# Narrow matmuls in a hybrid decoder trunk: value matmuls of two heads in alternate column halves, recurrence scores as 64x64 quarters

## The chip, the cores and the metric

The kernel runs on one core of one Trainium2 chip. The metric is the device time of one execution in microseconds; the kernel before takes 1604.14 us (median of 3 runs, 1604.09 to 1604.67). A core has a matmul engine (TensorE, PE in the profile, with its weight loads as PEld), three engines for elementwise work (VectorE is DVE, ScalarE is ACT, GpSimd is POOL) and DMA queues, here issued by SyncE (SP). TensorE's array has 128 rows and 128 columns; a matmul loads a stationary operand ("weights") and streams a moving one past it, and writes to PSUM, which the other engines then read.

## The reference

Two layers over 256 tokens of width 1024, batch 1, all in float32. Each layer is: x = LN(a x + half SwiGLU); x = LN(a x + W_o sum of three gated mixers); x = LN(a x + attention over 256 memory tokens); x = LN(a x + half SwiGLU). The three mixers share one input projection:

- A, native sparse attention: 8 heads of 64 channels in two key groups; compressed, selected and sliding branches. At 256 tokens all blocks of the selection and the whole window are in reach, so selected and sliding are two causal attentions with keys and values of their own.
- B, a gated linear recurrence (HGRN2) with 4 heads of 128 channels: out(t) = sum over s <= t of a(t, s) v(s), with a(t, s) = sum over channels of q(t) k(s) exp(b(t) - b(s)), where b is the running sum of the logarithms of the forget gates.
- C, multi-head latent attention with 8 heads, causal.

The change concerns the scores a(t, s) of B, and the sums of weights times values of A and C:

```
a = einsum('bhtd,bhtsd,bhsd->bhts', qt, decay, kt);  intra = einsum('bhts,bhse->bhte', a, vt)
o_sel = einsum('bgtrkl,bgtkld->bgtrd', p, vg);  o_win = einsum('bnqgrk,bnkgd->bnqgrd', p_w, vwb)
o (MLA) = einsum('bhqk,bkhd->bqhd', p, v)
```

## The kernel before

Tokens are two tiles of 128 (NT = 2, S = 256). The large projections multiply split operands in three float32r matmuls each (`mm3`, lines 126 to 129); the small matmuls of the mixers are plain float32, which the chip runs as two passes, so that the trace has two weight loads and two matmuls for each of them. Weights stream in from memory in blocks (`wblock`) and are split into a high and a low part by ScalarE (line 77) and VectorE (line 78).

The order of work is not the order of the text. The program is written down once in textual order, and a planner (line 1201) then orders each engine's queue with a timing model: it sends what is ready, and of several ready instructions the textually first. Instructions of the text can thus be sent ahead of others that wait. Semaphores follow from the tiles' uses. Buffers come from pools: m4 ("big", 10 tiles of 4 KB per partition), m2 ("half", 8 of 2 KB), PSUM pools `pw` and `acc` of 4 banks each, and the tag "pT" with 2 buffers.

`mixer` (from line 461) runs the recurrence first. `fT`, `kT`, `qT` hold gates, keys and queries with channels on partitions. Scores inside blocks of four tokens are made first (lines 579 to 584): for each token tile and head a 128x128 matmul `lv`, multiplied by a mask into `at[t]`, which holds scores with keys on partitions and queries along the row. Then `level(i, m)` for m = 4, 8, 16, 32, 64 (lines 596 to 612) adds the pairs of neighbouring blocks of m tokens: again 8 matmuls of 128x128, each token tile copied under a mask (line 604), then keys and queries are multiplied by the block's decay for the next level. Level 4 follows the masks at once; each of the other levels stands behind one more projection (`proj_nat`, PSUM name `pn`). Pairs between the two token tiles are one more product, `atx` (line 664). `hgrn_out` multiplies `at` and `atx` with the values.

The attention of A and C goes in 12 units (lines 928 to 955): 8 heads of A with their two branches, then 4 units of C with two heads each. A unit runs some filler units (projections of gates and branches, PSUM names `mg` and `br`; the counts are `FILLS`, line 34), turns the weights of its head or heads (`flip`, six transposes of p into PSUM name `pt`, copied to the two halves of pT by ScalarE, line 448, and VectorE, line 450), computes scores and softmax of the unit two ahead (`soften_a`, `soften_c`), and then applies its own weights to the values with `weigh` (line 453): per branch or head two matmuls with 64 columns of weights (the values), one with 256 streaming columns (line 454) and one with 128 (line 455). Their output is 64 partitions of a PSUM tile of 128: even heads write partitions 0 to 63, odd heads 64 to 127, and so use the left or the right half of the array's columns. The accumulator `oa` of two heads is started by line 824 (the compressed branch, 128 columns); `oc` is that of C.

Of the kernel before, what the change touches and what calls it, by code (L numbers as in the profile page):

```python
# [12 lines left out]
I32 = mybir.dt.int32  # L13
U8 = mybir.dt.uint8
AF = mybir.ActivationFunctionType
# [19 lines left out]
LEVELS = (4, 8, 16, 32, 64)  # L35
C_ID, C_CAUS, C_BASE, C_HM, C_CM, C_CM1, C_INV, C_END = 0, 128, 384, 512, 520, 552, 584, 600


@with_exitstack
def trunk(ctx, tc, a, out):  # L40
# [13 lines left out]
    def big(shape, dt=F32, name="m"):  # L54
        return m4.tile(shape, dt, tag="m4", name=name)

    def half(shape, dt=F32, name="h"):
        return m2.tile(shape, dt, tag="m2", name=name)
# [21 lines left out]

    # weights that a LayerNorm's work on the same engines must not wait for
    held = []
# [60 lines left out]

# [1 line left out]
    cst = const.tile([P, C_END], F32, name="cst")  # L145
    msk = const.tile([P, 5, P], U8, name="msk")
    ident = cst[:, C_ID:C_ID + P]
    caus = cst[:, C_CAUS:C_CAUS + S]
    basem = cst[:, C_BASE:C_BASE + P]
    headm = cst[:, C_HM:C_HM + 8]  # L150
# [7 lines left out]
    def load_constants():  # L158
        nc.sync.dma_start(cst, a["cst"])
        mski = big([P, 5, P], I32, name="mski")  # L160
        nc.sync.dma_start(mski, a["msk"])
        V.tensor_copy(msk, mski)
        nc.sync.dma_start(vec, a["vec"])
        nc.sync.dma_start(w2k, a["w2k"])
        nc.sync.dma_start(w2v, a["w2v"])

# [1 line left out]
    def xT_tiles():  # L168
# [19 lines left out]

    # matmuls whose results nobody reads, so that the clock of TensorE is up when there is work again
    def warm(n, x):  # L190
# [13 lines left out]

# [1 line left out]
    cc16 = const.tile([P, NT, 16], F32, name="cc16")  # L206
# [46 lines left out]

# [1 line left out]
    lbt = const.tile([P, DEPTH, 4], F32, name="lbt")  # L255
# [24 lines left out]

# [1 line left out]
    def layer_norm(ys, l, i, last=False, idle=0):  # L282
# [55 lines left out]

# [1 line left out]
    def ffn(l, i, xT, first=None, then=(), pre=()):  # L340
# [53 lines left out]

# [1 line left out]
    def mem_k(l, memT, K32, c, w=None):  # L396
# [18 lines left out]

# [1 line left out]
    def soft(score, scale, gate=None):  # L417
# [34 lines left out]

    def weigh(o, v, pT, start):
        T.matmul(o, v[0], pT[:, 0:S], start=start, stop=False, skip_group_check=True)
        T.matmul(o[:, P:S], v[1], pT[:, S:S + P], start=False, stop=True, skip_group_check=True)

    kc_blk = const.tile([P, 2, 32], F32, name="kc_blk")
    V.memset(kc_blk, 0.0)

# [1 line left out]
    def mixer(l, xT, first, pre):  # L461
# [28 lines left out]

        # gated sum of the branch projections, in units of one weight block
        order = "bac"
# [48 lines left out]

        # HGRN2, channels on partitions
        fT, kT, qT = big([P, 4, S], name="fT"), big([P, 4, S], name="kT"), big([P, 4, S], name="qT")
# [15 lines left out]
        for h in range(4):  # L559
            ps = ppw([P, S], "zq")  # L560
            mode_b(ps, wblock(a["winb"][l, 4 + h]), xT)
            A.activation(qT[:, h, :], ps, AF.Copy)
        # sums of the logarithms within blocks of four tokens
        pairs = fT.rearrange("p h (n c) -> p (h n) c", c=2)
        V.tensor_tensor(pairs[:, :, 1:2], pairs[:, :, 1:2], pairs[:, :, 0:1], op=ALU.add)
        b4 = fT.rearrange("p h (n m) -> p (h n) m", m=4)
        V.tensor_tensor(b4[:, :, 2:4], b4[:, :, 2:4], b4[:, :, 1:2].to_broadcast([P, S, 2]), op=ALU.add)
        # pairs within those blocks, about the mean of the middle sums
        at = [half([P, 4, P], name="at") for _ in range(NT)]
        c2 = small([P, S], "c2")  # L570
# [7 lines left out]
        V.tensor_tensor(eq, eq, qT, op=ALU.mult)  # L578
        for t in range(NT):
            ps = ppw([P, 4, P], "lv")  # L580
            s = slice(t * P, (t + 1) * P)
            for h in range(4):
                T.matmul(ps[:, h, :], ek[:, h, s], eq[:, h, s], start=True, stop=True)
            V.tensor_tensor(at[t], ps, basem[:, None, :].to_broadcast([P, 4, P]), op=ALU.mult)
        # keys decayed to the end of their block, queries from the start of theirs, block by block twice as long
        dk = big([P, 4, S], name="dk")
# [9 lines left out]
        def level(i, m):  # L596
            nonlocal fm
            nb = 2 * S // m
            for t in range(NT):
                ps = ppw([P, 4, P], "lv")  # L600
                s = slice(t * P, (t + 1) * P)
                for h in range(4):
                    T.matmul(ps[:, h, :], kT[:, h, s], qT[:, h, s], start=True, stop=True)
                V.copy_predicated(at[t], msk[:, i, None, :].to_broadcast([P, 4, P]), ps)
            k3 = kT.rearrange("p h (n w m) -> p (h n) w m", w=2, m=m)
            q3 = qT.rearrange("p h (n w m) -> p (h n) w m", w=2, m=m)
            f3 = fm[:, 0:2 * nb].rearrange("p (n w) -> p n w", w=2)
            V.tensor_tensor(k3[:, :, 0, :], k3[:, :, 0, :], f3[:, :, 1:2].to_broadcast([P, nb, m]), op=ALU.mult)
            V.tensor_tensor(q3[:, :, 1, :], q3[:, :, 1, :], f3[:, :, 0:1].to_broadcast([P, nb, m]), op=ALU.mult)
            fm2 = small([P, S], "fm")  # L610
            V.tensor_tensor(fm2[:, 0:nb, None], f3[:, :, 0:1], f3[:, :, 1:2], op=ALU.mult)
            fm = fm2
# [3 lines left out]

        # NSA and MLA projections, tokens on partitions
        level(0, LEVELS[0])
# [40 lines left out]
        rsqrt(rkv, rkv, 1.0 / 256, RMS_EPS)  # L659
        # pairs between the two token tiles  # L660
        atx = half([P, 4, P], name="atx")
# [4 lines left out]

        # compressed keys and values
        ct = big([P, 4, S], name="ct")
# [36 lines left out]
        def hgrn_out(t):  # L705
            ps = ppw([P, 4, P], "ob")
            for h in range(4):
                hs = slice(h * P, (h + 1) * P)
                if t == 1:
                    T.matmul(ps[:, h, :], atx[:, h, :], vN[:, 0, hs], start=True, stop=False)  # L710
                T.matmul(ps[:, h, :], at[t][:, h, :], vN[:, t, hs], start=(t == 0), stop=True)
            ob = wk.tile([P, 4, P], F32, tag="p", name="obn")
# [63 lines left out]

        # queries and keys with channels on partitions
        qtu = big([P, 4, S], name="qtu")
# [25 lines left out]

        # selected and sliding attention, both at once for every head
        yah, yal = y_tiles("a")

        def soften_a(h):
# [9 lines left out]
            return soft(score, 1.0, gt[:, :, h, 1:3])  # L818

        def values_a(h, pT):  # L820
            j, r = h // 2, slice(h % 2 * 64, h % 2 * 64 + 64)
            if h % 2 == 0:
                oa[j] = pacc([P, S], "oa")
                T.matmul(oa[j], vc[:, 2 * j:2 * j + 2, :].rearrange("p h d -> p (h d)"), pc, start=True, stop=False,
                         skip_group_check=True)
            for br in range(2):
                weigh(oa[j][r], [vs[:, t, br * 2 + h // 4, :] for t in range(NT)], pT[:, br], False)
            if h % 2 == 1:
                evac_hl(yah[:, j, :], yal[:, j, :], oa[j])

        oa = {}
        # MLA
        qm, kf, vm = [], [], []
# [66 lines left out]
        def values_c(u, pT):  # L900
            o = pacc([P, S], "oc")
            for w in range(2):
                weigh(o[w * 64:(w + 1) * 64], [vm[t][:, 2 * u + w, :] for t in range(NT)], pT[:, w], True)
            evac_hl(ych[:, u, :], ycl[:, u, :], o)

        # compressed attention's weights, both tiles and all heads at once
        scm = small([P, NT, 8, 16], "scm")
# [66 lines left out]

# [1 line left out]
    def cross(l, xT, memT, K32, vx, first, pre):  # L976
# [140 lines left out]
def _constants():  # L1117
# [3 lines left out]
    c[:, C_CAUS + P:C_CAUS + S] = np.where(i[None, :] <= i[:, None], 0.0, NEG)  # L1121
    c[:, C_BASE:C_BASE + P] = (i[:, None] // 4 == i[None, :] // 4) & (i[:, None] <= i[None, :])
    c[:, C_HM:C_HM + 8] = i[:, None] // 16 == np.arange(8)[None, :]
# [5 lines left out]
    c[:, C_INV:C_INV + 16] = np.float32(ROPE_THETA) ** (-np.arange(16, dtype=np.float32) / np.float32(16))  # L1129
    m = np.zeros((P, 5, P), np.int32)  # L1130
    for k, w in enumerate(LEVELS):
        same = i[:, None] // (2 * w) == i[None, :] // (2 * w)
        m[:, k, :] = same & (i[:, None] // w % 2 == 0) & (i[None, :] // w % 2 == 1)
    return c, m
# [79 lines left out]
```

## Time and profile before

| | |
|---|---|
| runs | 1604.14 us median, 1604.09 to 1604.67 |
| profiled execution, first to last instruction (its own time as far as the profile shows it) | 1602.4 us |
| TensorE matmuls busy | 1583.2 us, 99% |
| TensorE weight loads busy | 1462.7 us, 91% |
| VectorE / ScalarE busy | 1046.2 us, 65% / 826.8 us, 52% |
| mean granted TensorE clock | 0.998 |
| DMA | 282.49 MB, mean 176 GB/s |

The profile is one execution. Records of matmuls overlap, since they are pipelined: the record of a matmul is longer than its share of the array, and what it occupies is read from one start to the next. In a timeline, instructions of one kind that follow each other are merged into one row with their count (x16). "128*64 128x256" means 128 rows and 64 columns of weights, and an operand of 128 partitions with 256 elements (for a matmul the streaming one, for a weight load the stationary one).

### The profile page before, as it was taken

The page shows a single profiled execution, that of the slowest core. Times are in us where ns is not written, and L with a number is a line of the kernel's source. Part 1 is how long each engine was busy: PE and PEld are TensorE (multiplying, and loading weights), DVE is VectorE, ACT ScalarE, POOL GpSimd, SP SyncE. Part 2 cuts the span into 40 slices and gives each one's busy share as a digit, 9 for nine tenths or more (in the row PEclk, how much of TensorE's full clock was granted, in tenths as well). Part 3 has the DMA queues.
Part 4 walks back from the last instruction along what each step waited for, and adds up shares of the span by engine and source line. Part 5 has one row for each costly group of instructions (what it writes and reads, how often), then busy time and mean ns, then how long its engine had stood idle before and what let it go on. Part 6 is the DMA issues. An engine that isn't in the chain of part 4 may idle for free.

```text
span 1602.4 us, 27351 instructions
## 1 busy us (share of the span) xinstructions
PE 1583.2 (99%) x10896; PEld 1462.7 (91%) x10896; DVE 1046.2 (65%) x1831; ACT 826.8 (52%) x1396; POOL 32.8 (2%) x32
## 2 busy tenths in 40 slices
PE   9999999999999999999999999999999999999997
PEld 8999998898898989999999999988989989899996
DVE  5585559778766776555565555787786677655555
ACT  5455365566564564445444454745575545454443
POOL 0000000000000000000000000000000000000000
PEclk9999999999999999999999999999999999999999
DMA  8677455562555464566646676446525545556562
GB/s 292 210 221 261 136 171 159 164 225 67 165 169 181 132 215 151 186 198 222 212 124 189 201 215 206 131 152 192 193 77 155 164 158 179 176 172 184 184 186 77
DMA packets 81199, 282.49 MB, mean 176 GB/s; under 512 B 9392, under 2 KB 10544, under 8 KB 81072
## 3 DMA queue, kind: packets, MB, share of 16 engines
q1 hardware_dynamic: 81072, 280.75, 55.1%
q8 instruction: 85, 1.39, 0.4%
q14 instruction: 42, 0.34, 0.1%
HBM read 279.67 MB, written 1.05 MB: 175 GB/s over the span
## 4 chain that ended last, share of the span: by engine, by line
PE 96%; DVE 1%; ACT 1%; DMA 1%; issue 0%; SPq 0%; POOLq 0%; POOL 0%; DVEq 0%; ACTq 0%
PE up L129 10%; PE up L127 10%; PE up L128 10%; PE y L127 7%; PE y L128 7%; PE y L129 7%; PE mg L127 3%; PE mg L128 3%; PE mg L129 3%; PE pn L127 3%; PE pn L128 3%; PE pn L129 3%; PE br L127 2%; PE br L129 1%; PE br L128 1%; PE up L138 1%
## 5 line engine op out<-in xcount | busy, mean ns | idle before, releaser
L78 DVE TENSOR_TENSOR wl<-raw,wh 128x1024 fp32r<-128x1024 f32 (+3 forms) x490 | 584.5, 1200 | 369.9 <-ACT wh L77 368.4
L77 ACT ACTIVATE wh<-raw 128x1024 fp32r<-128x1024 f32 (+3 forms) x490 | 504.6, 1039 | 517.1 <-issue 227.9
L127 PE MATMUL up<-xTh,wh 128*128 128x256 f32 x1360 | 384.8, 283 | 0.7 <-ACT xTh L77 0.6
L128 PE MATMUL up<-xTl,wh 128*128 128x256 f32 x1360 | 385.2, 284 | 0.0
L129 PE MATMUL up<-xTh,wl 128*128 128x256 f32 x1360 | 384.5, 283 | 0.0
L127 PEld LDWEIGHTS up<-xTh,wh 128*128 128x128 f32 x1360 | 260.8, 192 | 4.8 <-ACT xTh L77 1.3
L128 PEld LDWEIGHTS up<-xTl,wh 128*128 128x128 f32 x1360 | 260.9, 192 | 3.4 <-DVE xTl L78 0.4
L129 PEld LDWEIGHTS up<-xTh,wl 128*128 128x128 f32 x1360 | 260.7, 192 | 0.0
L128 PE MATMUL y<-wl,gh 128*128 128x512 f32 x352 | 137.3, 392 | 0.0
L127 PE MATMUL y<-wh,gh 128*128 128x512 f32 x352 | 136.9, 392 | 0.0
L129 PE MATMUL y<-wh,gl 128*128 128x512 f32 x352 | 135.7, 389 | 0.0
L127 PE MATMUL mg<-xTh,wh 128*128 128x256 f32 x384 | 110.1, 287 | 0.0
L128 PE MATMUL mg<-xTl,wh 128*128 128x256 f32 x384 | 109.5, 285 | 0.0
L129 PE MATMUL mg<-xTh,wl 128*128 128x256 f32 x384 | 108.8, 284 | 0.0
L129 PEld LDWEIGHTS y<-wh,gl 128*128 128x128 f32 x352 | 66.2, 188 | 14.3
L127 PEld LDWEIGHTS y<-wh,gh 128*128 128x128 f32 x352 | 66.4, 189 | 11.7
L128 PEld LDWEIGHTS y<-wl,gh 128*128 128x128 f32 x352 | 66.4, 189 | 10.9
L127 PEld LDWEIGHTS mg<-xTh,wh 128*128 128x128 f32 x384 | 73.5, 191 | 1.4 <-issue 1.4
L127 PE MATMUL pn<-wh,xTh 128*128 128x512 f32 (+1 forms) x192 | 74.3, 387 | 0.0
L129 PE MATMUL pn<-wh,xTl 128*128 128x512 f32 (+1 forms) x192 | 74.3, 387 | 0.0
L128 PE MATMUL pn<-wl,xTh 128*128 128x512 f32 (+1 forms) x192 | 74.3, 387 | 0.0
L128 PEld LDWEIGHTS mg<-xTl,wh 128*128 128x128 f32 x384 | 73.6, 192 | 0.4 <-issue 0.3
(406 smaller groups left out, 2879.7 us busy)
## 6 DMA issues: line engine op xcount, KB each, us to landing
raw<-in_w_dram SPq DMA_DIRECT2D x260, 512.0 KB, 4.2
raw<-in_winb_dram SPq DMA_DIRECT2D x64, 512.0 KB, 4.2
raw<-in_wina_dram SPq DMA_DIRECT2D x40, 512.0 KB, 3.7
raw<-in_wbr_dram SPq DMA_DIRECT2D x24, 512.0 KB, 4.3
raw<-in_wk_dram SPq DMA_DIRECT2D x16, 512.0 KB, 3.4
raw<-in_cw_dram SPq DMA_DIRECT2D x16, 512.0 KB, 4.2
raw<-in_wv_dram SPq DMA_DIRECT2D x16, 512.0 KB, 4.0
raw<-in_wq_dram SPq DMA_DIRECT2D x16, 512.0 KB, 4.4
```

Source lines behind the costliest of these rows:

```text
L77: i = A.activation(h, src, AF.Copy)
L78: j = V.tensor_tensor(l, src, f(h), op=ALU.subtract)
L127: T.matmul(o, lhs[0], rhs[0], start=start, stop=False)
L128: T.matmul(o, lhs[0], rhs[1], start=False, stop=False)
L129: latest[0] = T.matmul(o, lhs[1], rhs[0], start=False, stop=stop)
L138: T.matmul(o, w[i][:, k * P:(k + 1) * P], rhs[j][:, k], start=n + k == 0, stop=(n, k) == (2, nk - 1))
```

## The change

The values: `weigh` takes a list of two (output, values, weights) and issues the two 256-column matmuls, then the two 128-column ones. In A, `values_a` of an even head only keeps its pT; at the odd head the accumulator is started and both heads are weighed, branch by branch. In C the two heads of a unit are given to one `weigh`.

The recurrence: pairs inside 64 tokens are computed by `within` as matmuls of 64 keys by 64 queries. The two quarters on the diagonal of a 128x128 block go one after the other, with keys and output on partitions 0 to 63 and then 64 to 127 of one PSUM tile, for all 8 pairs of token tile and head. One masked operation then takes all of them (`near` is the right half of every block of `at`: for the upper partitions that is where these scores belong; for the lower ones the scores wait there). At the last level (m = 64) the lower partitions' scores are moved to the left half, and the pairs between the two 64-token halves (8 matmuls of 64x64, output on partitions 0 to 63) go to the right half. The left half of the upper partitions is set to zero. `at` becomes one tile of the big pool in place of two of the half pool. Masks and constants shrink.

```diff
-    def weigh(o, v, pT, start):
-        T.matmul(o, v[0], pT[:, 0:S], start=start, stop=False, skip_group_check=True)
-        T.matmul(o[:, P:S], v[1], pT[:, S:S + P], start=False, stop=True, skip_group_check=True)
+    def weigh(pair, start):
+        for o, v, pT in pair:
+            T.matmul(o, v[0], pT[:, 0:S], start=start, stop=False, skip_group_check=True)
+        for o, v, pT in pair:
+            T.matmul(o[:, P:S], v[1], pT[:, S:S + P], start=False, stop=True, skip_group_check=True)
...
-        at = [half([P, 4, P], name="at") for _ in range(NT)]
+        at = big([P, NT, 4, P], name="at")
+        V.memset(at[64:P, :, :, 0:64], 0.0)
+        near = at.rearrange("p t h s -> p (t h) s")[:, :, 64:P]
...
-        for t in range(NT):
-            ps = ppw([P, 4, P], "lv")
-            s = slice(t * P, (t + 1) * P)
-            for h in range(4):
-                T.matmul(ps[:, h, :], ek[:, h, s], eq[:, h, s], start=True, stop=True)
-            V.tensor_tensor(at[t], ps, basem[:, None, :].to_broadcast([P, 4, P]), op=ALU.mult)
+        def within(k, q):
+            ps = ppw([P, 8, 64], "lv")
+            for n in range(8):
+                for i in range(2):
+                    s = slice(n // 4 * P + i * 64, n // 4 * P + (i + 1) * 64)
+                    T.matmul(ps[i * 64:(i + 1) * 64, n, :], k[:, n % 4, s], q[:, n % 4, s], start=True, stop=True,
+                             skip_group_check=True)
+            return ps
+
+        V.tensor_tensor(near, within(ek, eq), basem[:, None, :].to_broadcast([P, 8, 64]), op=ALU.mult)
...
         def level(i, m):
-            for t in range(NT):
-                ps = ppw([P, 4, P], "lv")
-                s = slice(t * P, (t + 1) * P)
-                for h in range(4):
-                    T.matmul(ps[:, h, :], kT[:, h, s], qT[:, h, s], start=True, stop=True)
-                V.copy_predicated(at[t], msk[:, i, None, :].to_broadcast([P, 4, P]), ps)
+            if m < 64:
+                V.copy_predicated(near, msk[:, i, None, :].to_broadcast([P, 8, 64]), within(kT, qT))
+            else:
+                low = at[0:64].rearrange("p t h s -> p (t h) s")
+                V.tensor_copy(low[:, :, 0:64], low[:, :, 64:P])
+                ps = ppw([64, 8, 64], "lv")
+                for n in range(8):
+                    s = n // 4 * P
+                    T.matmul(ps[:, n, :], kT[:, n % 4, s:s + 64], qT[:, n % 4, s + 64:s + P], start=True, stop=True)
+                A.activation(low[:, :, 64:P], ps, AF.Copy)
...
+        wait = []
+
         def values_a(h, pT):
-            j, r = h // 2, slice(h % 2 * 64, h % 2 * 64 + 64)
+            wait.append(pT)
             if h % 2 == 0:
-                oa[j] = pacc([P, S], "oa")
-                T.matmul(oa[j], vc[:, 2 * j:2 * j + 2, :].rearrange("p h d -> p (h d)"), pc, start=True, stop=False,
-                         skip_group_check=True)
+                return
+            j = h // 2
+            oa = pacc([P, S], "oa")
+            T.matmul(oa, vc[:, 2 * j:2 * j + 2, :].rearrange("p h d -> p (h d)"), pc, start=True, stop=False,
+                     skip_group_check=True)
             for br in range(2):
-                weigh(oa[j][r], [vs[:, t, br * 2 + h // 4, :] for t in range(NT)], pT[:, br], False)
-            if h % 2 == 1:
-                evac_hl(yah[:, j, :], yal[:, j, :], oa[j])
+                weigh([(oa[i * 64:(i + 1) * 64], [vs[:, t, br * 2 + h // 4, :] for t in range(NT)], wait[i][:, br])
+                       for i in range(2)], False)
+            wait.clear()
+            evac_hl(yah[:, j, :], yal[:, j, :], oa)
...
-            for w in range(2):
-                weigh(o[w * 64:(w + 1) * 64], [vm[t][:, 2 * u + w, :] for t in range(NT)], pT[:, w], True)
+            weigh([(o[w * 64:(w + 1) * 64], [vm[t][:, 2 * u + w, :] for t in range(NT)], pT[:, w]) for w in range(2)], True)
```

## Rows read from the trace of the kernel before

**Rows 1.** The page: span, TensorE's busy time, and the chain that ended last, by engine.

```profile
span 1602.4 us, 27351 instructions
PE 1583.2 (99%) x10896; PEld 1462.7 (91%) x10896; DVE 1046.2 (65%) x1831; ACT 826.8 (52%) x1396; POOL 32.8 (2%) x32
...
PE 96%; DVE 1%; ACT 1%; DMA 1%; issue 0%; SPq 0%; POOLq 0%; POOL 0%; DVEq 0%; ACTq 0%
```

**Rows 2.** Busy time by stretch, first layer: the recurrence's levels, then the attention units.

```profile
255.00:310.00 55.00, 55.00 (x307) 48.69 (x306) 45.73 (x80) 24.63 (x43) 2.44 (x4) 1.00 0.52 158
366.00:490.00 124.00, 122.23 (x878) 109.06 (x877) 88.62 (x269) 73.13 (x183) 0.00 (x0) 1.00 0.43 132
```

**Rows 3.** The chain in order of time, 255 to 303, levels alone: start, us, what.

```profile
255.23 1.78 PE lv L583 x16
257.02 1.79 PE lv L603 x16
...
294.22 1.78 PE lv L603 x16
```

**Rows 4.** TensorE's timeline, values of head 0: start, us, engine, line, names, count.

```profile
380.46 0.65 PE L454 MATMUL oa<-pT,vs 128*64 128x256 f32 x2
380.94 0.38 PE L455 MATMUL oa<-pT,vs 128*64 128x128 f32 x2
381.16 0.59 PE L454 MATMUL oa<-pT,vs 128*64 128x256 f32 x2
381.59 0.38 PE L455 MATMUL oa<-pT,vs 128*64 128x128 f32 x2
381.91 0.70 PE L824 MATMUL oa<-pc,vc 128*128 128x256 f32 x2
```

**Rows 5.** TensorE's timeline, one head of C alone.

```profile
448.84 0.65 PE L454 MATMUL oc<-pT,vm 128*64 128x256 f32 x2
...
449.63 0.39 PE L127 MATMUL mg<-xTh,wh 128*128 128x256 f32 x1
449.85 0.28 PE L128 MATMUL mg<-xTl,wh 128*128 128x256 f32 x1
449.97 0.28 PE L129 MATMUL mg<-xTh,wl 128*128 128x256 f32 x1
```

**Rows 6.** TensorE's timeline, both heads of a unit of C together.

```profile
482.04 0.28 PE L129 MATMUL br<-yh,wl 128*128 128x256 f32 x1
482.25 0.66 PE L454 MATMUL oc<-pT,vm 128*64 128x256 f32 x4
482.73 0.40 PE L455 MATMUL oc<-pT,vm 128*64 128x128 f32 x4
483.06 0.39 PE L127 MATMUL br<-yh,wh 128*128 128x256 f32 x1
```

**Rows 7.** Weight loads of the same place, windows 482.20 to 482.27 and 482.40 to 483.10.

```profile
482.25 0.15 PEld L454 LDWEIGHTS oc<-pT,vm 128*64 128x64 f32 x2
...
482.52 0.37 PEld L455 LDWEIGHTS oc<-pT,vm 128*64 128x64 f32 x4
```

**Rows 8.** TensorE's timeline, float32 matmuls with 32 streaming columns.

```profile
366.11 0.97 PE L911 MATMUL psc<-kc_blk,qtu 128*128 128x32 f32 x8
366.92 0.36 PE L127 MATMUL mg<-xTh,wh 128*128 128x256 f32 x1
```

**Rows 9.** Instructions on tile lv: ns min/median/max, first and last start, forms.

```profile
L603 PEld LDWEIGHTS lv<-qT,kT x160: 187/192/193, 256.7 to 1087.5; 128*128 128x128 f32 x160
L604 DVE COPY_PREDICATED at<-msk,lv x20: 715/732/747, 259.9 to 1088.0; 128x512 f32<-128x512 uint8 x20
```

**Rows 10.** Instructions on tile pT.

```profile
L455 PEld LDWEIGHTS oc<-pT,vm x32: 136/137/138, 449.1 to 1278.3; 128*64 128x64 f32 x32
L448 ACT ACTIVATE pT<-pt x24: 469/486/491, 377.8 to 1273.8; 128x384 f32<-128x384 f32 x24
L450 DVE COPY pT<-pt x24: 523/553/559, 378.9 to 1274.2; 128x384 f32<-128x384 f32 x24
```

More of the change, by code (lines that the diff above doesn't have):

```diff
@@ L35 @@
 LEVELS = (4, 8, 16, 32, 64)
-C_ID, C_CAUS, C_BASE, C_HM, C_CM, C_CM1, C_INV, C_END = 0, 128, 384, 512, 520, 552, 584, 600
+C_ID, C_CAUS, C_BASE, C_HM, C_CM, C_CM1, C_INV, C_END = 0, 128, 384, 448, 456, 488, 520, 536
 @with_exitstack
@@ L145, in trunk @@
     cst = const.tile([P, C_END], F32, name="cst")
-    msk = const.tile([P, 5, P], U8, name="msk")
+    msk = const.tile([P, 4, 64], U8, name="msk")
     ident = cst[:, C_ID:C_ID + P]
     caus = cst[:, C_CAUS:C_CAUS + S]
-    basem = cst[:, C_BASE:C_BASE + P]
+    basem = cst[:, C_BASE:C_BASE + 64]
     headm = cst[:, C_HM:C_HM + 8]
@@ L159, in load_constants @@
         nc.sync.dma_start(cst, a["cst"])
-        mski = big([P, 5, P], I32, name="mski")
+        mski = big([P, 4, 64], I32, name="mski")
         nc.sync.dma_start(mski, a["msk"])
@@ L710, in hgrn_out @@
                     T.matmul(ps[:, h, :], atx[:, h, :], vN[:, 0, hs], start=True, stop=False)
-                T.matmul(ps[:, h, :], at[t][:, h, :], vN[:, t, hs], start=(t == 0), stop=True)
+                T.matmul(ps[:, h, :], at[:, t, h, :], vN[:, t, hs], start=(t == 0), stop=True)
             ob = wk.tile([P, 4, P], F32, tag="p", name="obn")
@@ L818, in soften_a @@
             return soft(score, 1.0, gt[:, :, h, 1:3])
+        wait = []
         def values_a(h, pT):
-            j, r = h // 2, slice(h % 2 * 64, h % 2 * 64 + 64)
+            wait.append(pT)
             if h % 2 == 0:
-                oa[j] = pacc([P, S], "oa")
-                T.matmul(oa[j], vc[:, 2 * j:2 * j + 2, :].rearrange("p h d -> p (h d)"), pc, start=True, stop=False,
-                         skip_group_check=True)
+                return
[3 more added lines that the diff above has]
+                     skip_group_check=True)
             for br in range(2):
-                weigh(oa[j][r], [vs[:, t, br * 2 + h // 4, :] for t in range(NT)], pT[:, br], False)
-            if h % 2 == 1:
-                evac_hl(yah[:, j, :], yal[:, j, :], oa[j])
-        oa = {}
+                weigh([(oa[i * 64:(i + 1) * 64], [vs[:, t, br * 2 + h // 4, :] for t in range(NT)], wait[i][:, br])
+                       for i in range(2)], False)
+            wait.clear()
+            evac_hl(yah[:, j, :], yal[:, j, :], oa)
         qm, kf, vm = [], [], []
@@ L1121, in _constants @@
     c[:, C_CAUS + P:C_CAUS + S] = np.where(i[None, :] <= i[:, None], 0.0, NEG)
-    c[:, C_BASE:C_BASE + P] = (i[:, None] // 4 == i[None, :] // 4) & (i[:, None] <= i[None, :])
+    r, q = i[:, None] % 64, np.arange(64)[None, :]
+    c[:, C_BASE:C_BASE + 64] = (r // 4 == q // 4) & (r <= q)
     c[:, C_HM:C_HM + 8] = i[:, None] // 16 == np.arange(8)[None, :]
@@ L1129, in _constants @@
     c[:, C_INV:C_INV + 16] = np.float32(ROPE_THETA) ** (-np.arange(16, dtype=np.float32) / np.float32(16))
[L1130 to L1133, printed above, removed]
+    m = np.zeros((P, 4, 64), np.int32)
+    for k, w in enumerate(LEVELS[:4]):
+        m[:, k, :] = (r // (2 * w) == q // (2 * w)) & (r // w % 2 == 0) & (q // w % 2 == 1)
     return c, m
```

## The prediction

> **What bounds the kernel now.** I read the page first. TensorE is busy for 99% of the span and the chain of work that ended last lies on it for 96% [rows 1]; the table by stretch says the same of the two stretches that the change touches: 55.0 of 55 us in the recurrence (255 to 310) and 122.2 of 124 us in the attention (366 to 490), while VectorE has 9 and 35 us of room there [rows 2]. The granted clock is 1.00 in both. So a microsecond of TensorE's queue taken out is a microsecond of the end, unless another engine becomes late. The question is then what the changed matmuls occupy, and for that "busy" is no use (records overlap); I go by starts: from one matmul's start to the next one's in the timeline.
>
> **Recurrence, before.** The chain shows one level (two token tiles, four heads, 16 passes of 128x128 with 128 streaming columns, since an f32 matmul is two passes) as 1.78 us, in a layer six times: first masks and level 4 back to back (3.57 us), then levels 8 to 64 alone [rows 3]. That is 0.111 us a pass. A layer spends 3.57 + 4 x 1.78 = 10.69 us.
>
> **What a visit to the narrow shape costs.** The value matmuls already use 64 columns. At 380.46 one head runs both branches in one go: two passes with 256 streaming columns take 381.59 - 381.16 = 0.43, two with 128 take 0.22 [rows 4]. So a pass costs 0.215 and 0.11, in proportion to its streaming columns, and a head's branch 0.65. But a single head and branch between wide matmuls occupies 449.63 - 448.84 = 0.79, 0.14 more, and the second wide matmul behind it comes 0.22 after the first instead of 0.12 [rows 5]; ahead of such a visit the first narrow one comes 0.21 after the wide one, not 0.12 [rows 6]. Entering and leaving cost 0.14 + 0.10 + 0.09 = 0.33 us per visit. One head and branch alone is thus 0.98, one head with both branches 1.45 (380.46 to 381.91) + 0.19 = 1.64.
>
> **What two halves cost together.** Once in a layer the planner has put both heads of a unit next to each other: at 482.25 four passes of 256 and four of 128, half of them in each column half, end at 483.06: 0.81 us, against 0.79 for one head alone [rows 5, 6]. Two halves run side by side at full rate. The weight loads do too: two loads, 137 ns each at this width, lie within 0.15 us [rows 7, 10].
>
> [...]
>
> **Part 1, levels as quarters.** Removed per level: 16 passes. Added: 16 matmuls of 64 columns by 64, 32 passes, alternating halves. No row shows a pass with 64 streaming columns and 64 of weights. By proportion (0.215, 0.11) it is 0.055; it can't be seen to be less. From above, the matmul with the fewest streaming columns, 32, takes 0.81 / 8 = 0.10 us, but with 128 columns of weights [rows 8]; a load of 64 is 192 - 137 = 55 ns shorter than one of 128 [rows 9, 10], so loads too go at about 0.055 for 64. I take 0.055, with halves side by side [rows 6]: 16 x 0.055 + 0.33 = 1.21 against 1.78. Masks and level 4 stay neighbours: 1.76 + 0.33 = 2.09 against 3.57. Level 64 becomes 8 matmuls in one half, 16 passes: 0.88 + 0.33 = 1.21 too. A layer: 2.09 + 4 x 1.21 = 6.93 against 10.69, 3.76 less; two layers **7.5 us**. Bounds: with no overlap 3.85 + 3 x 2.09 + 1.21 = 11.33, which is 1.3 us more in two layers; with 0.11 a pass and no overlap, the last rival.
>
> VectorE loses one of two masked copies of 0.73 us per level [rows 9] and gets a memset and a half-height copy; it has room and the end doesn't go by it: 0. `at` becomes one of the ten big tiles in place of two of the eight half tiles. I count nine big ones alive at the peak (`at`, qd twice, ct, st_cmp twice, vN, gN, th), so nothing waits: 0; if one did, the copy of a projection would come late by up to one level, 1.2 us a layer. The smaller mask and constant loads lie under the first feed-forward: 0.
>
> **Part 2, values in pairs.** The order is made by the planner, which sends any ready matmul when the textually first isn't. That decides this part. Before, a layer has 18 visits: of 11 for `oa` five are heads with both branches in one go and six a single branch, cut where the second branch's half of pT was not copied yet; of 7 for `oc` six are a single head and one is the pair [rows 4 to 6]. That makes 5 x 1.64 + 6 x 0.98 = 14.08 and 6 x 0.98 + 1.00 = 6.88 us a layer.
>
> After, the text has, per branch, first head 256, second head 256, first 128, second 128, all into one PSUM tile. In every visit of the trace the matmuls of one tile stand in textual order; if that holds, the first head's first matmul can be sent ahead alone (0.43 + 0.33 = 0.76), and the rest waits for the second head's pT. Per pair of heads:
> - one visit: 2 x 0.65 + 0.33 = 1.63;
> - cut between the branches: 2 x 0.98 = 1.96;
> - first matmul ahead, and cut between branches: 0.76 + 2 x 0.98 = 2.72.
> Heads 0 to 3 have no filler units between them and were mostly cut (heads 1 to 3): I take 2.72 for their two pairs. Heads 4 to 7 ran uncut, the last at 437.80: 1.96. Sum 9.36 against 14.08: 4.72 a layer, **9.4 us** in two. Bounds: 0 (order as before) and 2 x (14.08 - 6.52) = 15.1. For `oc` the three cut units give 0.76 + 0.98 = 1.74 each and the fourth 1.00: 6.22 against 6.88, **1.3 us** in two layers; bounds 0 and 2 x (6.88 - 4.00) = 5.8.
>
> The added wait: a pair holds both pT buffers, so the copies of the next head's flip (0.49 on ScalarE, 0.55 on VectorE [rows 10]) stand behind the pair's last matmul, and what is queued behind those copies (exponentials, weight splits) stands with them. TensorE has other matmuls to send meanwhile except in heads 0 to 3. Below, nothing; above, one such copy per pair in the first two pairs, 2 x 2 x 0.55 = 2.2 us. I take 0, as their 2.72 is already the worst cut.
>
> **Sum.** 7.5 + 9.4 + 1.3 = 18.2 us. The profiled span is 1602.4 [rows 1], the median of the runs 1604.1; the 1.7 between lies around the program and stays. 1604.1 - 18.2 = 1585.9.
>
> **Rivals.**
> - *The planner undoes the pairing*: the first head's four matmuls are all ready long before the second's and are sent into gaps, as before. For: L824 of the next pair is sent ahead at 381.91 already [rows 4]. Against: textual order within one PSUM tile in all visits. Only the levels count: 1604.1 - 7.5 = 1596.6.
> - *Pairing is perfect*: every pair in one visit: 7.5 + 15.1 + 5.8 = 28.4, 1575.7. For: both oa and oc have uncut visits. Against: six and six cut ones.
> - *Quarters run one after the other* though whole value matmuls don't: +1.3 - 10.7, 1594.7. Against: [rows 6, 7].
> - *Slower: a quarter pays load and stream in turn.* Place: `lv`; price 0.055 + 0.055 = 0.11 us for each of the 176 passes of a layer (32 twice, 32 three times, 16): 7.37 + 3 x 3.85 + 2.09 = 21.0 against 10.69, 20.6 more in two layers, less 10.7 from the values: 1614. It decides from 0.082 us a pass, where levels cost what the values give ((10.69 + 5.35 - 5 x 0.33) / 176). For: the passes of 0.10 with 32 columns [rows 8]. Against: loads under running matmuls [rows 7].
>
> **How the numbers follow.** Forecast and its neighbourhood (1581 to 1591) 0.50, perfect pairing 0.13, planner undoes it 0.15, quarters in turn 0.10, the slower one 0.06, something in the planner's order elsewhere 0.06, of which half within the bound. A measurement here tells 0.2%, 3.2 us, from no change. All but the slower rival and half of the last are below 1600.9. That makes faster 0.90, same 0.04, slower 0.06. The range, 1577 to 1599, leaves out part of the perfect pairing and the slow side.
>
> **What would show it.** Levels: 32 passes in starts about 1.05 us wide, two starts within 0.02 us, and the next projection matmul after them; about 3.5 us between two such starts would be the slower rival. Values: visits of eight or sixteen passes with 454 of both halves together, fewer than 18 a layer; 18 visits and passes of one half alone mean that the planner undid it. VectorE's masked copies halve. I am wrong if the attention stretch is no shorter although its visits are, because TensorE idles on pT or p.

## The result and the profile after

The changed kernel takes 1585.06 us (median of 4 runs, 1584.85 to 1585.19) against 1604.41 us for the kernel before, run beside it: a ratio of 0.9879 with a 95% interval of 0.9865 to 0.9893. The prediction said 1585.9 us, a gain of 18.2; the gain is 19.35 us in the medians and 1602.4 - 1583.4 = 19.0 us in the span.

The page of the kernel after, where [rows 1] stood before: span, busy time by engine, and the chain that ended last.

```profile
span 1583.4 us, 27651 instructions
PE 1565.3 (99%) x11056; PEld 1445.4 (91%) x11056; DVE 1038.0 (66%) x1821; ACT 828.2 (52%) x1398; POOL 34.4 (2%) x32
...
PE 97%; DVE 1%; ACT 1%; issue 0%; DMA 0%; POOLq 0%; POOL 0%; DVEq 0%; SPq 0%; ACTq 0%
```

TensorE has 160 matmuls more, is busy for 17.9 us less, and is still what bounds the kernel. The stretches of [rows 2], after (length, then busy time of PE, PEld, DVE, ACT, POOL, granted clock, DMA share, GB/s):

```profile
255.00:310.00 55.00, 55.00 (x401) 46.32 (x401) 45.00 (x80) 26.18 (x44) 2.38 (x4) 1.00 0.56 169
366.00:490.00 124.00, 122.62 (x926) 111.09 (x925) 94.46 (x282) 78.69 (x191) 0.00 (x0) 1.00 0.44 142
```

In the same 124 us TensorE starts 48 instructions more and VectorE 13 more: TensorE is as full as it was, and the work has moved forward beneath it. The clock is the same. The chain of waits, 255 to 303, levels alone, where [rows 3] stood (start, us, what):

```profile
255.43 2.02 PE lv L589 x64
...
266.29 1.08 PE lv L589 x32
...
291.56 1.08 PE lv L616 x16
```

A level is 32 passes in 1.08 us instead of 16 in 1.78 us; masks and level 4 together are 2.02 instead of 3.57. TensorE's timeline around one level (start, us, engine, line, names, count):

```profile
265.90 0.39 PE L128 MATMUL pn<-wl,xTh 128*128 128x512 f32 x1
266.22 1.15 PE L589 MATMUL lv<-qT,kT 128*64 128x64 f32 x32
267.30 0.50 PE L129 MATMUL pn<-wh,xTl 128*128 128x512 f32 x1
267.63 0.39 PE L127 MATMUL pn<-wh,xTh 128*128 128x512 f32 x1
267.86 0.40 PE L128 MATMUL pn<-wl,xTh 128*128 128x512 f32 x1
```

It is entered 0.32 us after the wide matmul ahead of it and left over 0.33, where the wide ones follow each other by 0.23: the two switches cost 0.09 + 0.10 outside the 1.08. So a level occupies 1.08 + 0.2 = 1.28 us; the prediction had 1.21.

The values of heads 0 and 1, in the timeline where [rows 4] stood. Line 456 is the part with 256 streaming columns, 458 the part with 128, line 446 the transposes of the next heads' weights:

```profile
377.27 0.65 PE L456 MATMUL oa<-pT,vs 128*64 128x256 f32 x2
377.85 0.70 PE L841 MATMUL oa<-pc,vc 128*128 128x256 f32 x2
...
380.04 0.43 PE L456 MATMUL oa<-pT,vs 128*64 128x256 f32 x1
380.05 0.43 PE L458 MATMUL oa<-pT,vs 128*64 128x128 f32 x2
...
380.84 0.55 PE L446 MATMUL pt<-cst,p 128*128 128x128 f32 x3
381.32 0.43 PE L456 MATMUL oa<-pT,vs 128*64 128x256 f32 x1
381.32 0.43 PE L458 MATMUL oa<-pT,vs 128*64 128x128 f32 x2
```

These are the three visits that the forecast gave this pair: the first matmul ahead by itself (377.27), then eight passes (380.04 to 380.84), then, after a cut for the second branch's half, the last six (381.32). A unit of C, where [rows 5] stood with one head:

```profile
442.01 0.65 PE L456 MATMUL oc<-pT,vm 128*64 128x256 f32 x4
442.49 0.39 PE L458 MATMUL oc<-pT,vm 128*64 128x128 f32 x4
442.81 0.38 PE L127 MATMUL mg<-xTh,wh 128*128 128x256 f32 x1
```

Both heads take 442.81 - 442.01 = 0.80 us, what one head took alone. In a layer there are now 9 visits for `oa` instead of 11 and 6 for `oc` instead of 7.

### The profile page after: what moved, and what is told of

It reads as the page before. It is cut to its first block, busy times and chain, and to the rows that moved or that the text cites. A ratio compares the mean times of both kernels' runs of the same rounds, so it can differ in the third digit from the quotient of the medians.

```text
span 1583.4 us, 27651 instructions
## 1 busy us (share of the span) xinstructions
PE 1565.3 (99%) x11056; PEld 1445.4 (91%) x11056; DVE 1038.0 (66%) x1821; ACT 828.2 (52%) x1398; POOL 34.4 (2%) x32
## 4 chain that ended last, share of the span: by engine, by line
PE 97%; DVE 1%; ACT 1%; issue 0%; DMA 0%; POOLq 0%; POOL 0%; DVEq 0%; SPq 0%; ACTq 0%
PE up L127 10%; PE up L128 10%; PE up L129 10%; PE y L127 7%; PE y L128 7%; PE y L129 7%; PE mg L127 3%; PE mg L128 3%; PE mg L129 3%; PE pn L127 3%; PE pn L128 3%; PE pn L129 3%; PE br L127 2%; PE br L129 1%; PE br L128 1%; PE up L138 1%
```

## The experiments

Gains are given against the kernel before in runs on the same chip. Diffs are against the changed kernel unless it is said otherwise.

**One part alone.** The first kernel, e1_levels, has the levels as quarters, and `weigh`, `values_a` and `values_c` as before:

```diff
...
-        for o, v, pT in pair:
-            T.matmul(o, v[0], pT[:, 0:S], start=start, stop=False, skip_group_check=True)
-        for o, v, pT in pair:
-            T.matmul(o[:, P:S], v[1], pT[:, S:S + P], start=False, stop=True, skip_group_check=True)
+        T.matmul(o, v[0], pT[:, 0:S], start=start, stop=False, skip_group_check=True)
+        T.matmul(o[:, P:S], v[1], pT[:, S:S + P], start=False, stop=True, skip_group_check=True)
...
```

The second, e2_values, has the values in pairs, and the levels with their masks and tiles as before:

```diff
...
-                V.copy_predicated(near, msk[:, i, None, :].to_broadcast([P, 8, 64]), within(kT, qT))
...
+                V.copy_predicated(at[t], msk[:, i, None, :].to_broadcast([P, 4, P]), ps)
...
```

> The recurrence's quarters alone; the values are weighed head by head as before. Theory (each part gives what its visits to TensorE become shorter, and nothing flows back): by starts in the two traces a layer's levels go from 10.7 us to 2.02 + 4 x 1.08 + 5 x 0.2 = 7.3, so 2 x 3.4 = 6.8 us faster, about 1597.6. Rival (the time of the shorter levels is lost again, as the projections around them wait for weights, and the gain came from the values): 1603 to 1604.5.

> The paired values alone; the levels are 128x128 as before. Theory: the visits of oa go from 14.1 to 9.5 us a layer and those of oc from 6.9 to 5.4, so 2 x 6.1 = 12.1 us faster, about 1592.3, and with the levels' 6.8 this adds up to the whole change. Rival (heads 0 to 3 have no other work on TensorE, so that shorter visits there only make it wait for p or pT): 4 to 5 us less is gained, about 1597.

Levels alone: 1597.82 us (1597.33 to 1598.49), ratio 0.9960 (0.9948 to 0.9973), 6.4 us less. Values alone: 1591.74 us (1591.26 to 1592.37), ratio 0.9923 (0.9911 to 0.9936), 12.5 us less. Together 18.9, against 19.35 for both in one kernel: within half a microsecond the parts add, and neither hides the other. By stretch they add without a rest: the recurrence is as long in the first kernel, and the attention in the second, as in the changed kernel (60.9 and 155.4 us; the stretches are those of the next section). A level in the chain of the first, then of the second:

```profile
266.61 1.08 PE lv L587 x32
```

```profile
267.96 1.78 PE lv L605 x16
```

**Do the two column halves overlap because neighbours alternate?** The same quarters, with all of the left half first.

```diff
-            for n in range(8):
-                for i in range(2):
+            for i in range(2):
+                for n in range(8):
```

> The changed kernel, but each set of quarters is issued with all eight left ones first and then all eight right ones, so that 16 passes of one column half stand in the queue before the first of the other. Theory A (the two halves of the array take their matmuls independently, from far down the queue): no change, 1585 within 1 us, and the starts of a level still span 1.08 us. Theory B (halves overlap only when they stand next to each other in the queue): each of the five sets of a layer takes 16 x 0.058 = 0.93 us longer, 9.3 us in all, about 1594.4, and a level's starts span about 2.0 us.

It took 1592.50 us (1591.91 to 1592.70), ratio 0.9927 (0.9914 to 0.9939): 7.4 us above the changed kernel. Both theories missed: order matters, but the halves aren't wholly in turn either. Its levels in the chain:

```profile
255.79 3.34 PE lv L589 x64
267.96 1.83 PE lv L589 x32
```

Two sets of 16 passes strictly in turn would hold 32 x 0.058 = 1.86 us of streams and the 0.15 that a visit has beside them (1.08 - 16 x 0.058), 2.01; in step they take 1.08. At 1.83 the right half runs 1.83 - 1.08 = 0.75 us late, which is 13 passes of 0.058, not 16. How full the halves are shows in the matmuls of this line, by stretch (length, busy time of PE and of PEld with the number under way, granted clock, DMA share, GB/s): first this kernel, then the changed one.

```profile
267.85:268.64 0.79, 0.74 (x12) 0.75 (x13) 1.00 0.64 214
268.64:268.83 0.19, 0.19 (x10) 0.19 (x9) 1.00 0.86 333
```

```profile
266.20:266.64 0.44, 0.42 (x14) 0.42 (x16) 1.00 0.96 376
```

For 0.79 us one half works alone and gets through twelve passes, where the changed kernel has fourteen under way in 0.44; then, with four of the left half's 16 to go, the right half joins. So here a matmul of the other column half starts ahead of its place in the order, but only by about four passes. The place of before where both heads stood together [rows 6] fits: there four passes of the first head stood ahead of the second head's in the text, and the second head's began at once with them. Those four are 0.65 us of streams, four of these 0.23, so in these two places it goes by the number of passes rather than by their time.

**Is the reach four passes?** Blocks of two and of four blocks of tokens per half (4 and 8 passes), which a reach of four forecasts differently.

```diff
-            for n in range(8):
-                for i in range(2):
+            for g, i in [(g, i) for g in range(0, 8, 2) for i in range(2)]:
+                for n in range(g, g + 2):
```

(e9_blocks4 has 4 in place of 2.)

> The changed kernel, but the quarters alternate in blocks of two matmuls (four passes) of one half. With a reach of four passes (in the run with all left ones first the first right pass started with the left one four places ahead of it) the halves overlap fully: a level's starts span 1.08 to 1.13 us and the time is 1585 to 1586. With overlap of direct neighbours alone a level takes about 1.25 us and the time is about 1587.

> As before it, in blocks of four matmuls (eight passes). Worked out with a reach of four passes and 0.058 us a pass, a level takes 1.18 + 0.15 to 0.20 = 1.33 to 1.38 us in place of 1.08, so 1585.1 + 10 x 0.28 = about 1588. With a reach of eight or more it would stay at 1585; with direct neighbours alone 1.7 us a level, about 1591.

Blocks of two: 1585.28 us (1585.09 to 1585.76), ratio 0.9882 (0.9866 to 0.9899), like strict alternation. Blocks of four: 1588.05 us (1587.94 to 1588.32), ratio 0.9899 (0.9884 to 0.9914), 3.0 us more. Both times are where a reach of four put them. Levels in their chains:

```profile
265.86 1.13 PE lv L589 x32
```

```profile
266.13 1.47 PE lv L589 x32
```

The level of 1.47 is 0.1 us longer than the 1.33 to 1.38 worked out, and the runs don't place that rest. The reach itself shows in this kernel's matmuls of line 589, by stretch (columns as above): with blocks of eight passes four start alone in 0.29 us, and from the fifth on both halves run.

```profile
266.05:266.34 0.29, 0.28 (x4) 0.28 (x5) 1.00 0.17 61
266.34:266.46 0.12, 0.12 (x8) 0.12 (x7) 1.00 1.02 117
```

**What is alternation worth in the values?** Each head's two matmuls stand together again, the pair stays.

```diff
             T.matmul(o, v[0], pT[:, 0:S], start=start, stop=False, skip_group_check=True)
-        for o, v, pT in pair:
             T.matmul(o[:, P:S], v[1], pT[:, S:S + P], start=False, stop=True, skip_group_check=True)
```

> The changed kernel, but weigh issues the first head's two matmuls and then the second head's two, so that pairs stay together in the text and only the alternation inside a pair is gone. Theory A (what counts is that both halves have work in the same visit): only the cuts change, which makes the visits of a layer 10.1 us for oa and 6.9 for oc in place of 9.5 and 5.4: 2 x 2.1 = 4.2 us more than the whole change, about 1589.3. Theory B (without alternation the halves of a visit run in turn): 2 x 6 = 12 us more, about 1597, no better than the levels alone.

It took 1590.66 us (1590.30 to 1591.01), ratio 0.9916 (0.9903 to 0.9930): 5.6 us above the changed kernel, 1.4 more than the theory that only the cuts change. Theory B is refuted: where both heads meet, at 379.46, their eight passes take 0.80 us, as alternating ones do (442.81 - 442.01 in the changed kernel), and in e9_blocks2 blocks of four passes cost a level 1.13 us against 1.08 in strict alternation. The loss is in the cuts: with a whole head's matmuls ahead of the second head's, the planner sends all four passes of the first head's branch as soon as they are ready, and the two halves meet less often. That was in theory A's sum; of the 1.4 beyond it, 0.8 is idle time of TensorE in the attention (by the same stretch 1.77 us in a layer against 1.38 in the changed kernel), and the rest isn't placed. In C only one unit still runs as a pair; of the three visits of heads 0 and 1 only the middle one has both halves (timeline):

```profile
376.68 0.65 PE L456 MATMUL oa<-pT,vs 128*64 128x256 f32 x2
377.17 0.38 PE L457 MATMUL oa<-pT,vs 128*64 128x128 f32 x2
...
379.46 0.66 PE L456 MATMUL oa<-pT,vs 128*64 128x256 f32 x4
379.94 0.40 PE L457 MATMUL oa<-pT,vs 128*64 128x128 f32 x4
380.26 0.55 PE L446 MATMUL pt<-cst,p 128*128 128x128 f32 x3
380.74 0.65 PE L456 MATMUL oa<-pT,vs 128*64 128x256 f32 x2
381.23 0.38 PE L457 MATMUL oa<-pT,vs 128*64 128x128 f32 x2
```

The first and the last are one head alone, 0.79 us each; in the changed kernel the first is two passes of 0.58 and the rest runs in pairs, but for the two left over. So it is the alternation in the text that keeps the planner from undoing the pairing in the changed kernel: only the first head's first matmul can be sent early, since the one behind it belongs to the second head.

**Can the cuts be avoided?** The planner sends the first head's matmul early because it stands first. Here the second head, whose weights come last, and the second branch stand first, so that a visit begins when all is ready.

```diff
-        for o, v, pT in pair:
+        for o, v, pT in pair[::-1]:
...
-            for br in range(2):
+            for br in (1, 0):
```

> The changed kernel with the order inside a pair reversed: weigh takes the second head first, and values_a the second branch first, so that the first narrow matmul of a pair is the one whose half of pT is copied last. If the matmuls of one PSUM tile keep the order of the text, none can be sent ahead alone, and the eight heads of A need 4 visits a layer (6.5 us) in place of 9 (9.5 us); C's units stay cut twice. Theory (cuts cost 0.33 us each and the lost overlap): 2 x 3.0 = 5.9 us less than the whole change, about 1579.2. Rival (in heads 0 to 3 TensorE then waits for p and pT, where the early matmul filled a gap): 1583 to 1587.

It took 1586.18 us (1584.95 to 1586.73), ratio 0.9886 (0.9871 to 0.9901): no gain. The visits came out as built, four of 1.45 us for `oa`, but TensorE now waits: it stands idle for 3.68 us of the attention in a layer, against 1.38 in the changed kernel. The timeline at head 1 (the last bracket is the idle time before an instruction and what ended it):

```profile
376.05 1.13 PE L841 MATMUL oa<-pc,vc 128*128 128x256 f32 x4 [0.97 <-DVE pc L951]
377.97 0.84 PE L446 MATMUL pt<-cst,p 128*128 128x128 f32 x6 [0.79 <-DVE p L438]
...
380.21 0.65 PE L456 MATMUL oa<-pT,vs 128*64 128x256 f32 x4
380.69 0.39 PE L458 MATMUL oa<-pT,vs 128*64 128x128 f32 x4
380.91 0.60 PE L456 MATMUL oa<-pT,vs 128*64 128x256 f32 x4
381.34 0.39 PE L458 MATMUL oa<-pT,vs 128*64 128x128 f32 x4
```

The visit that the changed kernel makes at 377.27 ran in a time when TensorE had nothing else to do: the transposes at 377.97 wait for VectorE's scaled weights (L438), and in the changed kernel, which came into the attention 0.6 us later, they start at 378.56, no later in the stage. TensorE waits in C, too: 0.67 us at 440.01, ahead of the first unit's values, until ScalarE has copied a half of pT (line 448), and 0.51 us at 471.95, until VectorE has (line 450).

**Only where nothing waits.** e7_order_by_unit keeps the order of e5 for all pairs of `oa`, but in C for the first and the last unit only (diff against e5):

```diff
-    def weigh(pair, start):
-        for o, v, pT in pair[::-1]:
+    def weigh(pair, start, late=True):
+        pair = pair[::-1] if late else pair
+        for o, v, pT in pair:
...
-        for o, v, pT in pair[::-1]:
+        for o, v, pT in pair:
...
-            weigh([(o[w * 64:(w + 1) * 64], [vm[t][:, 2 * u + w, :] for t in range(NT)], pT[:, w]) for w in range(2)], True)
+            weigh([(o[w * 64:(w + 1) * 64], [vm[t][:, 2 * u + w, :] for t in range(NT)], pT[:, w]) for w in range(2)], True,
+                  u == 0 or u == 3)
```

e10_first_pair puts the pair of heads 0 and 1 back in its natural order (diff against e7):

```diff
-            for br in (1, 0):
+            for br in (1, 0) if j else (0, 1):
...
-                       for i in range(2)], False)
+                       for i in range(2)], False, j > 0)
```

e11_fill moves one unit of filling work from ahead of head 0 to between heads 0 and 1, to fill the wait (diff against e7):

```diff
-FILLS = (7, 0, 0, 0, 1, 2, 2, 2, 4, 4, 4, 0)
+FILLS = (6, 1, 0, 0, 1, 2, 2, 2, 4, 4, 4, 0)
```

> As the reversed order, but for C the second head goes first only in its first and last unit. By the order that the planner makes of it C has 5 visits a layer in place of 6, and A 4. Theory: 2 x 3.7 = 7.4 us less than the whole change, about 1577.7. Rival (TensorE waits instead): 1583 to 1587.

> Second heads first as in e7_order_by_unit, but the pair of heads 0 and 1 keeps its natural order, so that its first matmul goes ahead alone. Theory: in e7 TensorE stood 1.17 us before the transposes of head 1 (as in e5, 376.80 to 377.97), and that early matmul, 0.57 us with its two passes, fills half of it; the price is one visit more, about 0.3 us a layer, so the time stays within 1 us of e7: 1582.5 to 1584.5 us. Rival: the whole of the wait goes because the order before head 1 was the cause of it: 2 x (1.17 - 0.34 - 0.3) = about 1 us below e7, 1582. Other rival: the cuts count in full, 2 x 1.09 = 2.2 us more than e7, 1585.6.

> e7_order_by_unit with one filler unit of the scan moved from in front of head 0 to between heads 0 and 1. Theory: TensorE's 1.17 us before the transposes of head 1 are a wait for the softmax of head 1 with nothing to run beside it; a unit of work there covers it, and the time falls by up to 2 x (1.17 - 0.34) = 1.7 us below e7: about 1581.8 us. Rival: the unit was covering the softmax of head 0, and the gap only moves in front of head 0: 1583 to 1585 us, no better than e7.

e7 took 1583.44 us (1582.48 to 1584.16), ratio 0.9869 (0.9855 to 0.9884): the rival's range, not the 1577.7 of the visits alone; TensorE's idle time in the attention is 3.16 us in a layer. e10 took 1583.29 us (1583.15 to 1584.05), ratio 0.9870 (0.9855 to 0.9885), with two visits more in a layer than e7 (its expectation said one) and within the range of its theory: the early matmul fills the wait, the idle time is 2.58 us, and the attention is 0.3 us longer than in e7. Its timeline, against the 0.79 us of idle time that e5 showed above:

```profile
376.39 0.70 PE L842 MATMUL oa<-pc,vc 128*128 128x256 f32 x2 [0.97 <-DVE pc L953]
377.02 0.65 PE L457 MATMUL oa<-pT,vs 128*64 128x256 f32 x2
377.60 0.70 PE L842 MATMUL oa<-pc,vc 128*128 128x256 f32 x2
378.31 0.85 PE L446 MATMUL pt<-cst,p 128*128 128x128 f32 x6
```

e11 took 1583.75 us (1582.61 to 1585.47), ratio 0.9870 (0.9853 to 0.9886), and tests nothing: the planner had sent the moved unit ahead of head 0 again, and the traces show TensorE's 11056 matmuls in the same order as in e7. It is a second set of runs of e7, and useful as one (last section).

e7 and e10 are some 1.7 us faster than the changed kernel by their medians, and by 2.8 and 2.1 us in the span (1580.6 and 1581.3). The intervals of the three ratios overlap, so that they are faster rests on the traces: from the first compressed scores (`psc`) to the next branch's first statistics (`pst`) a layer takes 154.3 us in e7, 154.5 in e10 and 155.4 in the changed kernel.

## Why the prediction was right

**What bounds it** held: TensorE is 99% busy before and after, and what its queue lost the end lost. The first layer shows where: from the first level to the first matmul into `hp` (line 732 before, 745 after) 64.35 us before and 60.90 after; from `psc` to `pst`, the attention with what follows it, 161.7 and 155.4. That is 3.45 + 6.25 in a layer, 19.4 in two; the rest of the program gave 0.4 back. Both stretches before, then both after (columns as in [rows 2]):

```profile
255.07:319.42 64.35, 64.35 (x347) 56.45 (x346) 51.89 (x87) 28.72 (x47) 2.44 (x4) 1.00 0.55 166
366.11:527.79 161.68, 159.91 (x1089) 142.18 (x1088) 116.71 (x321) 89.54 (x208) 2.98 (x2) 1.00 0.45 141
...
255.36:316.26 60.90, 60.90 (x427) 51.49 (x427) 47.77 (x81) 28.42 (x47) 2.38 (x4) 1.00 0.58 176
362.92:518.35 155.43, 154.05 (x1089) 137.99 (x1088) 116.21 (x321) 89.96 (x208) 2.99 (x2) 1.00 0.45 146
```

**Levels**: 7.5 predicted, 6.9 by those stretches, 6.4 in e1. A pass was taken as 0.055 us and is 0.058; the two switches and what a visit has inside were 0.33 and are 0.15 + 0.2 = 0.35. With five visits a layer (masks and level 4 are one) that is 2.02 + 3 x 1.08 + 1.08 + 5 x 0.2 = 7.34 against the 6.93 forecast. Side by side, the term on which it all hung, was right, on a condition that the prediction met without naming it as one: the halves must alternate within a few passes (a level takes 1.08 us in strict alternation, 1.13 in blocks of four passes, 1.47 in blocks of eight and 1.83 in blocks of sixteen; e9, e3).

**Values, `oa`**: 9.4 predicted. Nine visits of together 7.82 us replace eleven of 11.99, and two switches of 0.2 go: 4.57 a layer, 9.1. The rule that the planner keeps the matmuls of one PSUM tile in textual order held, though not its grounds: the prediction read it from starts, and in its own [rows 6] the second head's passes of line 454 start ahead of the first head's of line 455. That fits the reach of about four passes that e3 and e9 showed, which it didn't know. The first matmul went ahead alone in three of the four pairs, and the first two pairs ran as the three visits of 2.72 that the working gave them (0.58 + 0.80 + 0.80 + 3 x 0.2 = 2.78). The other two were forecast with one cut between the branches, 1.96 each; one ran whole (412.23, 1.45 + 0.2), one with its first matmul ahead (422.42 and 431.38, 0.58 + 1.44 + 2 x 0.2). That 4.07 is near 3.92 is luck.

**Values, `oc`**: 1.3 predicted, 2.9 measured: 4.34 us in six visits against 5.57 in seven, and one switch. This is the term that was mis-sized, by the number of cut units and not by their price. Three were expected to be cut; two were (470.95 and 474.75 start with the one matmul, and such a unit occupies 0.58 + 0.79 + 0.4 = 1.77, forecast 1.74), and two ran whole, as at 442.01.

**The added wait** at 0: there was none, and one went. TensorE stands idle for 161.68 - 159.91 = 1.77 us of the attention before and 155.43 - 154.05 = 1.38 after. What is missing after is the pause before line 127 here, where it stood until VectorE had copied a half of pT:

```profile
481.38 0.35 PE L127 MATMUL br<-yh,wh 128*128 128x256 f32 x1 [0.50 <-DVE pT L450]
```

e5 shows the price that was bounded above: where a pair begins late, the wait does come (3.68 us idle in the attention of a layer).

**Rivals.** The planner undoing the pairing and perfect pairing were both off; e4 shows the first one partly (a first head whose matmuls stand together is sent ahead), e5 to e7 the second (visits as few as that bring waits in return). Quarters in turn would have given 1594.7; e3, which comes near it, gives 1592.5. A quarter that pays load and stream one after the other (0.11 a pass) is refuted by 0.058. The 19.4 us of the two stretches are 1.2 more than the sum of 18.2: `oc` gave 1.6 more and the pause that went 0.8, the levels gave 0.6 and `oa` 0.3 less, and 0.3 of the difference isn't placed. That the total came so near is in part these errors cancelling.

VectorE's masked copies were forecast to halve and went from 20 to 8, as level 64 has none any more. In the same 55 us of the recurrence its busy time fell only from 45.73 to 45.00 us, since later work has moved up; from the first level to `hp` it fell from 51.89 to 47.77.

## What to carry to other kernels

Two matmuls that use half of the columns each shared TensorE's time here only where they stood within about four passes of each other in its queue (1.08 us a level in strict alternation, 1.83 with sixteen passes of one half first): write them alternately, and see to it that whatever orders the queue has no reason to send one half's matmuls ahead. Reckon a visit to a narrow shape as its streams plus about a third of a microsecond (0.35 us measured for a level), and count visits, not matmuls. The cut that filled a pause of the queue cost next to nothing, and removing it bought as little (e10 against e7: 0.3 us of 154).

## What the runs showed of the hardware

**Column halves took their work here with a reach of about four passes.** Strict alternation (two passes each) and blocks of four passes cost 1.08 and 1.13 us a level, blocks of eight 1.47, blocks of sixteen 1.83. Within the reach a matmul starts ahead of one that stands before it in the order: in e3 the right half's passes join after 0.79 us, with about four of the left half's 16 to go. The loads do too: e3's 32 loads of a level span 1.76 us, where one after the other, 0.058 apart, they would take 31 x 0.058 + 0.14 = 1.94. In the changed kernel `PEld` lists 132 to 138 ns for each, two every 0.058 us, under running matmuls of the same rows: from 266.20 to 266.64 the loads of line 589 and its matmuls are each busy for 0.42 of 0.44 us. It was so before: the loads of line 455 begin at 482.52, while the matmuls of line 454 run until 482.91 [rows 6, 7].

**Behind the same pauses, in the same order of work, one profiled run shows a lower granted clock and another doesn't.** e11 and e7 have the same order of matmuls. After the two pauses at head 1 (0.98 and 0.79 us idle in e11, 0.97 and 0.79 in e7), the granted clock of e11's profiled run is 0.56 over 3.80 us of the first layer and 0.50 over 3.00 us of the second; that of e7 stays at 1.00. By stretch, e11, then e7:

```profile
378.90:382.70 3.80, 3.76 (x17) 2.98 (x19) 3.01 (x16) 2.00 (x8) 0.00 (x0) 0.56 0.04 17
...
1161.20:1164.20 3.00, 2.96 (x12) 2.80 (x13) 2.47 (x11) 0.88 (x4) 0.00 (x0) 0.50 0.04 15
```

```profile
378.10:382.00 3.90, 3.65 (x30) 2.72 (x31) 3.05 (x16) 2.10 (x8) 0.00 (x0) 1.00 0.06 23
...
1159.30:1163.00 3.70, 3.53 (x30) 2.57 (x30) 2.97 (x16) 1.90 (x8) 0.00 (x0) 1.00 0.03 10
```

In 3.80 us of the one TensorE has 17 instructions under way, in 3.90 us of the other 30, and the attention takes 155.4 us against 154.3 (the spans are 1583.6 and 1580.6 us). The eight runs of this order fall in two groups, four from 1582.48 to 1582.89 us at a mean clock of 0.998 and four from 1584.10 to 1585.47 at 0.996 to 0.997; each group has two runs of e7 and two of e11. A lower clock may be part of what e5, with the same pauses, lost (1584.95 and 1585.81 us at 0.998, 1586.56 and 1586.73 at 0.997); e10 has only the first pause, shows 0.998 in all runs and lies mostly within 0.25 us (1583.15 to 1583.37, and one at 1584.05). That the second pause decides is argued from these, not shown by a run that changes the pause alone.
